# Two mixers and a routed expert layer on one core: attention in pairs of heads, a spread written four tokens at a time, and new places for urgent work in the first stage

## The chip, the core and the metric

One core of one Trainium2 chip runs the whole program. TensorE (PE) multiplies matrices into PSUM, VectorE (DVE) and ScalarE (ACT) work on elements, GpSimd (POOL) gathers rows here, and SyncE (SP) issues most DMAs. Each engine takes its instructions in the order in which they stand in the program. The metric is the time of one execution on the device in microseconds; less is better.

## What is computed

Two blocks over 512 tokens of width 1024, then a last norm in the first block's way of computing:

```python
# first block (rg_lru, peer: helpers)
ada = silu(c) @ w_ada + b_ada                     # sh1, sc1, g1, sh2, sc2, g2
h = rmsnorm(x) * (1 + sc1) + sh1
z = h @ w_in                                      # gate_b, gate_c, xa, xr, gr
y_a = gate_b * causal_dwconv(gate_c * xa)
y_b = rg_lru(causal_dwconv(xr), w_r, w_i, lambda) * gelu(gr)
x = x + g1 * (concat(head_rmsnorm(y_a), head_rmsnorm(y_b)) @ w_out)
x = x + g2 * peer(rmsnorm(x) * (1 + sc2) + sh2)   # 8 heads, the best 16 of 128*128 experts a head
x = rmsnorm(x)
# second block
h = rms_norm(x); proj = h @ w_in
moba = softmax(q k^T / 8 - slope * distance, causal) v * silu(a_z)   # 8 heads of 64
gdn = rms_norm(gated_delta_rule(silu(conv(q, k, v)), g, beta)) * silu(d_z)   # 4 heads of 128
x = x + rms_norm(concat(moba, gdn) @ w_out)
```

With 512 tokens and 3 selectable blocks of 256 keys every past block is selected, so the attention is plain causal attention.

## The kernel before

Large products are made in near fp32: `_split` (L98) copies a tile to fp32r on ACT (wH, hidH, yH, vH, cH) and takes the rest on DVE (wL, hidL, ...), and `_mm3` (L106) makes three matmuls of the parts. `_Weights` (L118) keeps two loaded chunks (wraw) and two split ones ahead. Instructions are put in order by a scheduler when the program is built; `tc.issue_after(x)` makes it keep an instruction behind x.

Stage 1 (`_phase1`, 0 to 217 us) holds x transposed, xT, as 8 chunks of 128 channels x 512 tokens. Squares (L265) are made on ACT and added on DVE (L268), `_token_sums` (ps_ts) sums them over channels on PE, rms and its reciprocal (L163, L164) follow, and four transposes (ps_row) spread it over the partitions. A column of the modulation is one DVE product with accumulation over a 128x1024 tile (wada, L218). xn (L298) is the normed x, hidH and hidL its parts, ps_zp the first product. Then come the convolutions, the gates (tanh, exp, sqrt on ACT, a scan on DVE), the head norms (hnr, rb, ps_row), the product with w_out into four banks at a time, the new xT (L432), and the second norm.

Routing (217 to 365 us) finds the best 16 keys of each head (`_top16` on DVE). Tokens 128 to 511 take the dense way: `spread` (365 to 549 us) makes, from one-hot tiles (ohA, ohB on DVE, L640), a 128x128 table of coefficients for each token on PE (ps_g), ACT copies four tokens at a time into st (L663) and issues a DMA of st to gd in DRAM for every 32 tokens (L665). Beside it PE makes the first 46 of 128 chunks of the experts' inputs (psS, kept in ring). Then 128 steps follow (566 to 1430 us): g4, four chunks of gd for all tokens, is read back (L733), multiplied into ring (L741, DVE), split into cH and cL, and multiplied with the experts' rows (vraw, vH, vL) into pv (L749 to L755). In the first steps the scores of block 0, s, are loaded again (L763) and go through `_top16`.

The second mixer (1430 to 1810 us) weaves two generators of work: A makes the delta rule's inverses (ps_inv, ps_tm, ps_gr, ps_row) and its recurrence (ps_w, vn, ps_s, ps_o), B makes the projections (ps_p; aq, ak, av, az are the attention's), then the attention. PLAN says how many yields of A are woven with how many of B. `attention(j)` works on heads 2j and 2j+1, one after the other: logits ps_l, lg on DVE, exp on ACT, scaling; then for four key blocks transposes (ps_pT), a copy pT and the product ps_ao. G makes the gates of the delta rule and its norm. At the end comes the output projection (ps_m) and the last norm.

Of the kernel before, what the change touches and what calls it, by code (L numbers as in the profile page):

```python
# [20 lines left out]
P = 128  # L21
T = 512
D = 1024
KC = 8
# [6 lines left out]
GN = 4  # L31
LAG = 46
# [81 lines left out]
PLAN = [(18, 8), (18, 60), (12, 24)]  # L114
# [3 lines left out]
class _Weights:  # L118
# [103 lines left out]
def _phase1(k):  # L222

    nc, tc, I = k.nc, k.tc, k.I
    with tc.tile_pool(name="p1", bufs=1, reuse_waits="tile") as p1, \
# [11 lines left out]
        nc.scalar.activation(out=c1, in_=c1, func=AF.Silu)  # L237
        root = p1.tile([P, 1], F32, name="root")
        nc.scalar.activation(out=root, in_=k.eps, func=AF.Sqrt)
# [22 lines left out]
        def add_square(dc):  # L262
# [4 lines left out]
            if dc:  # L267
                nc.vector.tensor_tensor(out=sqs[0], in0=sqs[0], in1=sq, op=OP.add)  # L268

        def rms_row():  # L270

            r = tile_("rms", "rms", 2, (P, 4))
            _rstd(k, r, _token_sums(k, pps, [[sqs[0]]], "np", 2), 1.0 / D)
# [3 lines left out]
        for dc in range(KC):  # L277
            add_square(dc)
# [5 lines left out]
        rps = rms_row()  # L284
# [5 lines left out]
        for dc in range(KC):  # L290
            sc, sh = ada(1, dc), ada(0, dc)
# [5 lines left out]
            with tc.issue_after(mod.ins) if dc else ExitStack():  # L297
                nc.vector.scalar_tensor_tensor(out=t, in0=xT[:, dc, :], scalar=A, in1=row if dc else rps,  # L298
                                               op0=OP.mult, op1=OP.mult)
            with tc.issue_after(k.weights.last.ins) if dc else ExitStack():  # L300
                nc.scalar.activation(out=hH[:, dc, :], in_=t, func=AF.Identity, bias=sh)
# [6 lines left out]
        with tc.issue_after(mod.ins):  # L308
            kc_ = _softplus(k, p1, k.neglam, 4, "lru_k")
# [55 lines left out]
        for j in range(4):  # L365
            nc.scalar.activation(out=tt[j], in_=tt[j], func=AF.Sqrt)
# [13 lines left out]
        def headnorm(ys, gname, m0):  # L380
# [11 lines left out]
            for j, y in enumerate(ys):  # L392
# [4 lines left out]
                nc.vector.scalar_tensor_tensor(out=y, in0=y, scalar=k.col(gname, j, 1), in1=row,  # L397
                                               op0=OP.mult, op1=OP.mult)
# [17 lines left out]
        g1, sh2, sc2 = (ada_group(s, k.conv_end) for s in (2, 3, 4))  # L416
# [3 lines left out]
        for m in range(KC):  # L420
# [14 lines left out]
            add_square(m)  # L435
            xa.append(tile_("xa", ("gate0", "gate1")[m // 4], 4))
            nc.scalar.activation(out=xa[m], in_=xT[:, m, :], func=AF.Copy, scale=A2[:, m:m + 1])
        row = rms_row()
# [92 lines left out]
def _peer(k, psum):  # L531
# [10 lines left out]
    gd = k.dr.tile([NG, P, NK, GT], F32, name="gd")  # L542
# [25 lines left out]
    with ExitStack() as bctx:  # L568
# [63 lines left out]
        def spread(b, iT, gHL):  # L632
# [11 lines left out]
            for gq in range(P // GT):  # L644
                st = po.tile([P, NK, GT], F32, name="st", tag="st", bufs=2)
                for to in range(0, GT, OG):
# [9 lines left out]
                    for j0 in range(0, OG, 4):  # L656
# [73 lines left out]
    for c in range(NK):  # L730
        if c % GN == 0:
            g4 = pc.tile([P, NG, GN, GT], F32, name="g4", tag="g4", bufs=2)
            nc.sync.dma_start(out=g4, in_=gd[:, :, c:c + GN, :].rearrange("g p n t -> p g n t"))  # L733
# [61 lines left out]
def _mixer2(k, psum, pv):  # L795
# [138 lines left out]
    for tb in range(4):  # L934
        for hf in range(2):
# [3 lines left out]
            o = tile_("x3", "lg", 5)  # L939
# [164 lines left out]
    def attention(j):  # L1104
# [13 lines left out]
        nc.scalar.activation(out=az, in_=az, func=AF.Silu)  # L1118
        yield
        po = pps.tile([P, T], F32, name="ps_ao", tag="po", bufs=1)  # L1120
        for hh in range(2):
            h = 2 * j + hh
            off = hh * 64
            rows = slice(off, off + 64)
            slope = 2.0 ** -(h + 1)
            pr = []
            for qb in range(4):
                nk = (qb + 1) * P
# [3 lines left out]
                lg = tile_("lg", "lg", 5)  # L1132
                nc.vector.scalar_tensor_tensor(out=lg[:, 0:nk], in0=C["alibi"][:, 384 - qb * P:512], scalar=slope,
                                               in1=ps[:, 0:nk], op0=OP.mult, op1=OP.add)
                mx = p4.tile([P, 2], F32, name="mx", tag="mx", bufs=6)
                nc.vector.tensor_reduce(out=mx[:, 0:1], in_=lg[:, 0:nk], axis=AX.X, op=OP.max)
                nc.vector.tensor_scalar(out=mx[:, 0:1], in0=mx[:, 0:1], scalar1=-1.0, scalar2=None, op0=OP.mult)
                nc.scalar.activation(out=lg[:, 0:nk], in_=lg[:, 0:nk], func=AF.Exp, bias=mx[:, 0:1],
                                     accum_out=mx[:, 1:2])
                nc.vector.reciprocal(out=mx[:, 1:2], in_=mx[:, 1:2])  # L1140
                nc.vector.tensor_scalar(out=lg[:, 0:nk], in0=lg[:, 0:nk], scalar1=mx[:, 1:2], scalar2=None, op0=OP.mult)
                pr.append(lg)
                yield
            for kb in range(4):
                nq = (4 - kb) * P
                ps = pps.tile([P, T], F32, name="ps_pT", tag="pa", bufs=2)
                for qb in range(kb, 4):
                    nc.tensor.transpose(ps[:, (qb - kb) * P:(qb - kb + 1) * P], pr[qb][:, kb * P:(kb + 1) * P], k.ident)
                pT = tile_("pT", "pT", 3)
                if kb % 2:  # L1150
# [3 lines left out]
                nc.tensor.matmul(out=po[rows, kb * P:T], lhsT=av[:, kb, off:off + 64], rhs=pT[:, 0:nq],  # L1154
                                 start=kb == 0, stop=kb == 3)
                yield
        nc.vector.tensor_tensor(out=az, in0=az, in1=po, op=OP.mult)
        azs.append(az)

    zs = []  # L1160
# [47 lines left out]
    B = chain(delta_inputs(2, ins[1]), delta_inputs(3, ins[1]), *[attention(j) for j in range(4)])  # L1208
    for na, nb in PLAN:
        weave(A, na, B, nb)  # L1210
    for _ in A:
        pass
    G = chain(gates_of_delta(), gated_norm())
    weave(B, 200, G, 10)
# [186 lines left out]
```

## Time and profile before

| | us |
|---|---|
| median of 3 runs | 1864.59 |
| lowest, highest | 1864.06, 1872.85 |
| the profiled execution | 1863.24 |
| its span, first to last instruction | 1861.5 |
| PE busy | 1777.6 (95%) |
| DVE busy | 1480.4 (80%) |
| ACT busy | 831.2 (45%) |

PE is the busiest engine, and its rests are short and of many causes; one of 17.2 us stands out, before the 128 steps. A matmul that streams slowly counts as busy, so the share says nothing of how dense the work is. The clock granted to PE was 0.984 of full speed in the mean.

### The profile page before, as it was taken

How to read it: one execution, taken by the hardware profiler on the slowest of the kernel's cores; microseconds unless marked ns; L12 is line 12 of the kernel's file. 1: busy time of each engine (PE TensorE's matmuls, PEld its weight loads, DVE VectorE, ACT ScalarE, POOL GpSimd, SP SyncE). 2: the span in 40 equal slices, each digit the busy share in tenths (PEclk: the TensorE clock that was granted, in tenths of full speed). 3: DMA queues.
4: the chain of work that ended last, by engine and by line, in shares of the span. 5: the costliest groups of instructions: out<-in, count | busy, mean ns of one | idle time of the engine just before them, and what ended most of it. 6: DMA issues, size and time to landing. Idle time of an engine off the chain costs nothing.

```text
span 1861.5 us, 26283 instructions
## 1 busy us (share of the span) xinstructions
PE 1777.6 (95%) x9613; PEld 1542.2 (83%) x9613; DVE 1480.4 (80%) x3012; ACT 831.2 (45%) x1188; POOL 333.7 (18%) x260
## 2 busy tenths in 40 slices
PE   6999898999968999999999999999999999999988
PEld 5777688999957999999999999988887788767768
DVE  7788699999989978888887888898965774566665
ACT  4464534367863433333333333333335753454452
POOL 0000000000000044544444444455400000000000
PEclk9999999999978999999999999999999999999999
DMA  8355333345669789999999999999962311111022
GB/s 307 124 178 208 121 111 108 122 173 215 259 236 284 235 300 372 356 355 331 346 335 342 334 334 349 336 331 345 352 245 76 112 69 58 57 46 46 12 79 91
DMA packets 153414, 404.53 MB, mean 217 GB/s; under 512 B 12098, under 2 KB 64578, under 8 KB 151748
## 3 DMA queue, kind: packets, MB, share of 16 engines
q1 hardware_dynamic: 114690, 243.45, 38.0%
q0 software_dynamic: 36864, 134.23, 19.8%
q10 hardware_dynamic: 1730, 25.17, 3.5%
q8 instruction: 75, 1.23, 0.3%
q14 instruction: 55, 0.45, 0.1%
HBM read 370.30 MB, written 32.51 MB: 216 GB/s over the span
## 4 chain that ended last, share of the span: by engine, by line
PE 84%; DVE 11%; ACT 3%; issue 1%; DMA 1%; DVEq 0%; ACTq 0%; SPq 0%
PE pv L749 10%; PE pv L752 9%; PE pv L755 9%; PE psS L110 8%; PE psS L109 8%; PE psS L108 8%; PE ps_p L109 3%; PE ps_p L108 3%; PE ps_p L110 3%; PE ps_zp L110 2%; PE ps_zp L109 2%; PE ps_zp L108 2%; PE ps_inv L952 2%; DVE wL L102 2%; PE ps_g L660 2%; DVE ohB L640 1%
## 5 line engine op out<-in xcount | busy, mean ns | idle before, releaser
L101 ACT ACTIVATE wH<-wraw 128x1024 fp32r<-128x1024 f32 x204 | 216.4, 1062 | 417.0 <-PE psS L109 257.8
L108 PE MATMUL psS<-hidH,wH 128*128 128x384 f32 x1024 | 346.9, 339 | 3.5 <-ACT ring L554 3.5
L110 PE MATMUL psS<-hidH,wL 128*128 128x384 f32 x1024 | 346.6, 339 | 3.4 <-DVE wL L102 3.4
L109 PE MATMUL psS<-hidL,wH 128*128 128x384 f32 x1024 | 346.6, 338 | 0.0
L102 DVE TENSOR_TENSOR wL<-wraw,wH 128x1024 fp32r<-128x1024 f32 x204 | 248.9, 1221 | 88.7 <-ACT wH L101 88.3
L707 POOL DMA_INDIRECT row<-uN,uidx x128 | 166.4, 1300 | 831.2 <-DVE cL L102 659.0
L749 PE MATMUL pv<-vH,cH 128*128 128x512 f32 x768 | 223.6, 393 | 17.2 <-ACT vH L101 17.2
L755 PE MATMUL pv<-vH,cL 128*128 128x512 f32 x768 | 237.5, 390 | 0.0
L752 PE MATMUL pv<-vL,cH 128*128 128x512 f32 x768 | 237.4, 390 | 0.0
L101 ACT ACTIVATE cH<-ring 128x384 fp32r<-128x384 f32 x128 | 67.2, 526 | 323.0 <-PE pv L752 301.4
L108 PEld LDWEIGHTS psS<-hidH,wH 128*128 128x128 f32 x1024 | 193.4, 189 | 7.7 <-ACT ring L554 4.5
L716 POOL DMA_INDIRECT row<-vR,vidx x128 | 167.1, 1306 | 172.9 <-DVE acc L722 140.8
L110 PEld LDWEIGHTS psS<-hidH,wL 128*128 128x128 f32 x1024 | 193.3, 189 | 5.2 <-DVE wL L102 4.9
L109 PEld LDWEIGHTS psS<-hidL,wH 128*128 128x128 f32 x1024 | 193.3, 189 | 3.2
L749 PEld LDWEIGHTS pv<-vH,cH 128*128 128x128 f32 x768 | 143.7, 189 | 42.3 <-ACT vH L101 17.4
L709 DVE SCALAR_TENSOR_TENSOR row<-row,h2tok 128x1024 f32<-128x1024 f32 x128 | 154.9, 1220 | 25.5 <-DMA row<-uN,uidx 25.4
L722 DVE SCALAR_TENSOR_TENSOR acc<-row,act,acc 128x1024 f32<-128x1024 f32 x127 | 162.6, 1280 | 11.5 <-DMA row<-vR,vidx 10.7
L102 DVE TENSOR_TENSOR vL<-vraw,vH 128x1024 fp32r<-128x1024 f32 x128 | 156.2, 1221 | 18.5 <-ACT vH L101 18.3
L752 PEld LDWEIGHTS pv<-vL,cH 128*128 128x128 f32 x768 | 144.1, 188 | 31.1
L755 PEld LDWEIGHTS pv<-vH,cL 128*128 128x128 f32 x768 | 144.1, 188 | 31.0
L101 ACT ACTIVATE vH<-vraw 128x1024 fp32r<-128x1024 f32 x128 | 135.8, 1061 | 0.4 <-DMA vraw<-vR 0.2
L663 ACT ACTIVATE st<-ps_g 128x512 f32<-128x512 f32 x96 | 96.2, 1145 | 32.3 <-PE ps_g L660 31.7
(415 smaller groups left out, 2973.0 us busy)
## 6 DMA issues: line engine op xcount, KB each, us to landing
wraw<-uT SPq DMA_DIRECT2D x128, 512.0 KB, 5.9
vraw<-vR SPq DMA_DIRECT2D x128, 512.0 KB, 6.6
wraw<-w_in SPq DMA_DIRECT2D x52, 512.0 KB, 3.5
wada<-wada SPq DMA_DIRECT2D x48, 512.0 KB, 4.9
gd<-st ACTq DMA_DIRECT2D x12, 2048.0 KB, 7.3
g<-gd SPq DMA_DIRECT2D x32, 768.0 KB, 9.2
wraw<-w_out SPq DMA_DIRECT2D x16, 512.0 KB, 3.6
wraw<-w_q SPq DMA_DIRECT2D x8, 512.0 KB, 3.5
```

The source lines that it names most:

```text
L101: copy = nc.scalar.activation(out=H, in_=src, func=AF.Copy)
L102: nc.vector.tensor_tensor(out=L, in0=src, in1=H.bitcast(F32), op=OP.subtract)
L108: nc.tensor.matmul(out=ps, lhsT=lH, rhs=rH, start=start, stop=False)
L109: nc.tensor.matmul(out=ps, lhsT=lH, rhs=rL, start=False, stop=False)
L110: nc.tensor.matmul(out=ps, lhsT=lL, rhs=rH, start=False, stop=stop)
L707: nc.gpsimd.indirect_dma_start(out=row, out_offset=None, in_=I["uN"], in_offset=bass.IndirectOffsetOnAxis(ap=uidx[:, n:n + 1], axis=0))
L709: nc.vector.scalar_tensor_tensor(out=row, in0=row, scalar=1.0, in1=h2tok, op0=OP.mult, op1=OP.mult, accum_out=act0[:, n:n + 1])
L716: nc.gpsimd.indirect_dma_start(out=row, out_offset=None, in_=k.vrows, in_offset=bass.IndirectOffsetOnAxis(ap=vidx[:, n:n + 1], axis=0))
L722: nc.vector.scalar_tensor_tensor(out=k.acc0, in0=row, scalar=act0[:, n:n + 1], in1=k.acc0, op0=OP.mult, op1=OP.add)
L749: nc.tensor.matmul(out=pv[b][h], lhsT=cH[:, bs], rhs=vH[:, h * 512:(h + 1) * 512], start=first, stop=False)
L752: nc.tensor.matmul(out=pv[b][h], lhsT=cH[:, bs], rhs=vL[:, h * 512:(h + 1) * 512], start=False, stop=False)
L755: nc.tensor.matmul(out=pv[b][h], lhsT=cL[:, bs], rhs=vH[:, h * 512:(h + 1) * 512], start=False, stop=last)
```

## The change

In the first stage silu goes ahead of the square root's first use, softplus goes behind the last hidH, the first weights are loaded and split (`first`) before the modulation's first two columns, which wait for the last addition of squares, and each further pair of columns waits for the xn before (`scaled`). At the end of the stage the last square is no longer added on DVE: its sums over channels are made by matmuls of their own and added as 128x4. The gates' r and i use two kinds of banks, gelu waits for the last sqrt and has four buffers, and of the last three groups of modulation columns the third (sh2) waits for the last head norm.

In the spread st is written with four neighbouring tokens in its innermost dimension. gd becomes two tensors, of the first 16 chunks and of the other 112, with a DMA for each. In the second mixer the attention works on both heads of a pair at once, in three generators: the projections, the softmax, and the values, which are woven with the next pair's projections. The last pair's values are woven with the gates. The logits have tiles of their own size.

```diff
-PLAN = [(18, 8), (18, 60), (12, 24)]
+PLAN = [(18, 8), (18, 56), (12, 20)]
...
+    def first(self):
+
+        self.load()
+        self.split()
...
-        def rms_row():
+            if 0 < dc <= last:
+                return nc.vector.tensor_tensor(out=sqs[0], in0=sqs[0], in1=sq, op=OP.add)
+
+        def rms_row(last):
...
+            sums = _token_sums(k, pps, [[q] for q in sqs[0:1] + sqs[last + 1:]], "np", 2)
+            if last < KC - 1:
+                nc.vector.tensor_copy(out=r, in_=sums[:, 4:8])
+                nc.vector.tensor_tensor(out=r, in0=r, in1=sums[:, 0:4], op=OP.add)
+                sums = r
+            _rstd(k, r, sums, 1.0 / D)
...
-        rps = rms_row()
+        k.weights.first()
+        with tc.issue_after(added.ins):
+            for s in (1, 0):
+                ada(s, 0)
+        rps = rms_row(KC - 1)
...
+            if dc < KC - 1:
+                with tc.issue_after(scaled.ins):
+                    for s in (1, 0):
+                        ada(s, dc + 1)
...
-            H, L = k.weights.get()
+            with tc.issue_after(scaled.ins):
+                H, L = k.weights.get()
...
-        with tc.issue_after(mod.ins):
+        with tc.issue_after(mod.ins), tc.issue_after(high.ins):
             kc_ = _softplus(k, p1, k.neglam, 4, "lru_k")
...
-                ps = bank("gp", 2)
+                ps = bank(("gp", "np")[g], 2)
...
-                g = tile_("gg", "gg", 2)
-                nc.scalar.activation(out=g, in_=ps, func=AF.Gelu_apprx_tanh)
+                g = tile_("gg", "gg", 4)
+                with tc.issue_after(gate.ins):
+                    nc.scalar.activation(out=g, in_=ps, func=AF.Gelu_apprx_tanh)
...
-        g1, sh2, sc2 = (ada_group(s, k.conv_end) for s in (2, 3, 4))
+        g1, sc2, sh2 = (ada_group(s, after) for s, after in ((2, k.conv_end), (4, k.conv_end), (3, k.normed)))
...
-    gd = k.dr.tile([NG, P, NK, GT], F32, name="gd")
+
+    gd = [k.dr.tile([NG, P, n, GT], F32, name="gd%d" % n) for n in (NF, NK - NF)]
...
-                        nc.scalar.activation(out=st[:, :, o:o + 4].rearrange("p n t -> p t n"), in_=ps,
+                        nc.scalar.activation(out=st[:, :, o:o + 4], in_=ps.rearrange("p t n -> p n t"),
                                              func=AF.Copy, scale=1.0 / GSCALE)
-                nc.scalar.dma_start(out=gd[(b - 1) * (P // GT) + gq], in_=st)
+                for part, cs in zip(gd, (slice(0, NF), slice(NF, NK))):
+                    nc.scalar.dma_start(out=part[(b - 1) * (P // GT) + gq], in_=st[:, cs, :])
...
+            src, c0 = (gd[0], c) if c < NF else (gd[1], c - NF)
+            nc.sync.dma_start(out=g4, in_=src[:, :, c0:c0 + GN, :].rearrange("g p n t -> p g n t"))
...
+    def values(j, st):
+        aq, ak, av, az, pr = st[j]
+        po = pps.tile([P, T], F32, name="ps_ao", tag="po", bufs=1)
+        for kb in range(4):
+            nq = (4 - kb) * P
+            pts = []
+            for hh in range(2):
...
+                pts.append(pT)
+            yield
+            for rows, pT in zip(halves, pts):
+                nc.tensor.matmul(out=po[rows, kb * P:T], lhsT=av[:, kb, rows], rhs=pT[:, 0:nq],
                                  start=kb == 0, stop=kb == 3)
...
+    def attention():
+
+        st = {}
+        yield from projections(0, st)
+        for j in range(4):
+            yield from softmax(j, st)
+            if j < 3:
+                a, b = values(j, st), projections(j + 1, st)
+                for n in range(5):
+                    next(a)
+                    yield
+                    next(b)
+                    yield
...
-    weave(B, 200, G, 10)
+    weave(last[0], 9, G, 9)
```

How the instructions move is shown at three places. The first is DVE at the start of stage 1, from the fifth addition of squares on; sq_100 is the sum, A a column of the scale. Before:

```order
L268 TENSOR_TENSOR sq_100<-sq_100,sq_117 128x512
L218 SCALAR_TENSOR_TENSOR wada,ada<-wada,cb 128x1024
L268 TENSOR_TENSOR sq_100<-sq_100,sq_120 128x512
L218 SCALAR_TENSOR_TENSOR wada,ada<-wada,cb 128x1024
L294 SCALAR_TENSOR_TENSOR A_142<-ada,cols,G_123 128x1
L292 TENSOR_TENSOR ada<-ada,cols 128x1
L102 TENSOR_TENSOR wL<-wraw,wH 128x1024
L164 RECIPROCAL rms<-rms 128x4
L102 TENSOR_TENSOR wL<-wraw,wH 128x1024
L218 SCALAR_TENSOR_TENSOR wada,ada<-wada,cb 128x1024
L298 SCALAR_TENSOR_TENSOR xn<-xT,A_142,ps_row 128x512
```

And now:

```order
L275 TENSOR_TENSOR sq_100<-sq_100,sq_117 128x512
L275 TENSOR_TENSOR sq_100<-sq_100,sq_120 128x512
L103 TENSOR_TENSOR wL<-wraw,wH 128x1024
L224 SCALAR_TENSOR_TENSOR wada,ada<-wada,cb 128x1024
L170 RECIPROCAL rms<-rms 128x4
L310 SCALAR_TENSOR_TENSOR A_156<-ada,cols,G_123 128x1
L224 SCALAR_TENSOR_TENSOR wada,ada<-wada,cb 128x1024
L308 TENSOR_TENSOR ada<-ada,cols 128x1
L314 SCALAR_TENSOR_TENSOR xn<-xT,A_156,ps_row 128x512
```

The additions are no longer parted by a wada product, the reciprocal of rms comes behind one wL and one wada, and one wada product stands between it and xn.

The second is PE in the mixer, at the stretch from 1665 us on in the trace before, where the second head's products of one pair (ps_ao), the next logits (ps_l) and the inputs of a new group of inverses (ps_row, ps_gr) meet. Before:

```order
L182 MATMUL ps_row<-ca,gcum 128x128 x4
L182 MATMUL ps_row<-ca,ksc 128x128 x4
L1154 MATMUL ps_ao<-pT,av 64x256
L1130 MATMUL ps_l<-ak,aq 128x128
L966 MATMUL ps_gr<-kT 128x128 x4
L1154 MATMUL ps_ao<-pT,av 64x128
L1130 MATMUL ps_l<-ak,aq 128x256
L1130 MATMUL ps_l<-ak,aq 128x384
L182 MATMUL ps_row<-ca,ksc 128x128 x4
L966 MATMUL ps_gr<-kT 128x128 x4
L1130 MATMUL ps_l<-ak,aq 128x512
L108 MATMUL ps_p<-hidH,wH 128x512
```

And now, at the same group of inverses:

```order
L188 MATMUL ps_row<-ca,ksc 128x128 x4
L1194 MATMUL ps_ao<-pT,av 64x512 x2
L1184 MATMUL ps_pT<-ca,lg 128x128
L991 MATMUL ps_gr<-kT 128x128 x4
L1184 MATMUL ps_pT<-ca,lg 128x128 x5
L110 MATMUL ps_p<-hidL,wH 128x512
L111 MATMUL ps_p<-hidH,wL 128x512
L109 MATMUL ps_p<-hidH,wH 128x512
L110 MATMUL ps_p<-hidL,wH 128x512
L111 MATMUL ps_p<-hidH,wL 128x512
```

Projections (ps_p) now stand between the products of the attention, and the two ps_ao of a pair stand next to each other.

The third is PE at the first step of the delta rule's recurrence, near 1780 us in the trace before. Before:

```order
L952 MATMUL ps_inv<-kv,XT 128x128 x4
L952 MATMUL ps_inv<-XT,kv 128x128 x4
L1075 MATMUL ps_w<-S,nwT 128x128 x3
L1148 MATMUL ps_pT<-ca,lg 128x128 x2
L1075 MATMUL ps_w<-S,nwT 128x128
L1148 MATMUL ps_pT<-ca,lg 128x128 x2
L1083 MATMUL ps_s<-vn,ik 128x128 x4
```

And now:

```order
L984 MATMUL ps_tm<-ca,vT 128x128 x4
L1194 MATMUL ps_ao<-pT,av 64x128 x2
L977 MATMUL ps_inv<-kv,XT 128x128 x4
L977 MATMUL ps_inv<-XT,kv 128x128 x4
L1100 MATMUL ps_w<-S,nwT 128x128 x4
L1108 MATMUL ps_s<-vn,ik 128x128 x4
L1115 MATMUL ps_o<-S,qT 128x128
```

The transposes of the last softmax no longer stand between the steps of the recurrence; they are woven with the gates ahead of it.

## Rows read from the trace of the kernel before

**Rows 1.** Table of stretches: PE, weight loads, DVE, ACT, POOL busy us; clock; DMA.
```profile
365.00:530.00 165.00, 165.00 (x1367) 156.10 (x1366) 156.72 (x313) 122.52 (x143) 0.00 (x0) 1.00 0.57 210
530.00:550.00 20.00, 12.25 (x116) 9.73 (x114) 19.25 (x47) 15.32 (x17) 0.00 (x0) 0.68 0.61 245
550.00:566.00 16.00, 0.26 (x1) 0.26 (x2) 10.31 (x60) 2.21 (x4) 0.00 (x0) 0.50 0.83 296
...
1663.00:1720.00 57.00, 52.05 (x276) 38.32 (x277) 36.25 (x86) 24.18 (x44) 0.00 (x0) 1.00 0.14 47
1720.00:1810.00 90.00, 81.95 (x514) 61.59 (x513) 58.96 (x138) 45.44 (x83) 0.00 (x0) 1.00 0.13 42
```

**Rows 2.** Who waited for whom, PE: us in total, times, longest.
```profile
PE pv L749 <- ACT vH L101: 17.2, 1, 17.2
PE ps_ts L156 <- DVE sq L268: 8.3, 2, 5.4
...
PE ps_zp L108 <- ACT hidH L301: 3.3, 1, 3.3
...
PE ps_p L108 <- DVE aq L1106: 2.5, 1, 2.5
PE ps_pT L1148 <- DVE lg L1141: 2.2, 2, 1.8
...
PE ps_row L182 <- ACT rb L394: 1.6, 1, 1.6
```

**Rows 3.** Timeline of PE, start: start, us, what, in brackets idle before.
```profile
22.54 2.07 PE L108 MATMUL ps_zp<-hidH,wH 128*128 128x512 f32 x4 [3.30 <-ACT hidH L301]
```

**Rows 4.** Timeline of DVE, start.
```profile
14.81 0.68 DVE L268 TENSOR_TENSOR sq<-sq,sq 128x512 f32<-128x512 f32 x1
...
17.90 0.17 DVE L164 RECIPROCAL rms<-rms 128x4 f32<-128x4 f32 x1
```

**Rows 5.** Timeline of ACT, start.
```profile
6.30 1.28 ACT L209 ACT_TABLE_LOAD   x1
```

**Rows 6.** Timeline of PE near 115 us.
```profile
115.40 0.50 PE L108 MATMUL ps_zp<-hidH,wH 128*128 128x512 f32 x1 [1.53 <-ACT wH L101]
...
117.03 0.58 PE L110 MATMUL ps_zp<-hidH,wL 128*128 128x512 f32 x1 [0.90 <-DVE wL L102]
```

**Rows 7.** Timeline of DVE near 112 us, the first of three products.
```profile
112.32 1.21 DVE L218 SCALAR_TENSOR_TENSOR wada<-wada,cb 128x1024 f32<-128x1024 f32 x1
```

**Rows 8.** Who waited for whom, DVE, from 365 to 550 us.
```profile
DVE wL L102 <- ACT wH L101: 6.5, 7, 1.9
```

**Rows 9.** Costliest groups of the page: busy us, mean ns of one, idle before.
```profile
L663 ACT ACTIVATE st<-ps_g 128x512 f32<-128x512 f32 x96 | 96.2, 1145 | 32.3 <-PE ps_g L660 31.7
```

**Rows 10.** Timeline of ACT in the mixer, a plain copy.
```profile
1785.41 0.58 ACT L1153 ACTIVATE pT<-ps_pT 128x512 f32<-128x512 f32 x1
```

**Rows 11.** DMA queues from 550.5 to 555.6 us: packets, MB, share of 16 engines.
```profile
q10 hardware_dynamic: 128, 2.10, 108.8%
q1 hardware_dynamic: 15, 0.02, 0.8%
```

**Rows 12.** Timeline of DVE in the gap before the 128 steps.
```profile
558.17 0.49 DVE L455 MAX8 ts<-s 128x8 f32<-128x128 f32 x2 [4.29 <-DMA s<-sc]
...
563.16 1.50 DVE L741 TENSOR_TENSOR ring<-ring,g 128x384 f32<-128x384 f32 x3 [1.40 <-DMA g<-gd]
```

**Rows 13.** Timeline of DVE in the mixer, logits just ahead of aq.
```profile
1674.32 0.67 DVE L1133 SCALAR_TENSOR_TENSOR lg<-cb,ps_l 128x512 f32<-128x512 f32 x1
```

**Rows 14.** Timeline of PE in the recurrence, a step without other work.
```profile
1796.24 1.16 PE L1083 MATMUL ps_s<-vn,ik 128*128 128x128 f32 x8 [0.78 <-DVE vn L1078]
```

**Rows 15.** Groups of PE by line, 1430 to 1810 us.
```profile
L1130 PE MATMUL ps_l<-ak,aq 64*128 64x128 f32 (+3 forms) x64 | 23.6, 468 | 0.0
L1154 PE MATMUL ps_ao<-pT,av 128*64 128x512 f32 (+3 forms) x64 | 22.2, 451 | 1.6 <-ACT pT L1153 1.6
```

More of the change, by code (lines that the diff above doesn't have):

```diff
@@ L31 @@
 GN = 4
+NF = 16
 LAG = 46
@@ L236, in _phase1 @@
             nc.sync.dma_start(out=xT[:, 2 * q:2 * q + 2, :], in_=I["xT"][:, 2 * q:2 * q + 2, :])
-        nc.scalar.activation(out=c1, in_=c1, func=AF.Silu)
+        silu = nc.scalar.activation(out=c1, in_=c1, func=AF.Silu)
         root = p1.tile([P, 1], F32, name="root")
-        nc.scalar.activation(out=root, in_=k.eps, func=AF.Sqrt)
+        with tc.issue_after(silu.ins):
+            nc.scalar.activation(out=root, in_=k.eps, func=AF.Sqrt)
         nc.scalar.dma_start(out=k.cd, in_=c1)
@@ L260, in _phase1, with add_square @@
         sqs = []
-        def add_square(dc):
+        def add_square(dc, last):
             sq = tile_("sq8", ("th", "gc")[dc // 4], 4)
@@ L277, in _phase1 @@
         for dc in range(KC):
[L278 removed]
+            added = add_square(dc, KC - 1)
         G1 = p1.tile([P, 8], F32, name="G1")
@@ L1102, in recurrence, with projections @@
             yield
-    def attention(j):
+    def projections(j, st):
         aq, ak = tile_("aq", "aq", 2), tile_("ak", "ak", 2)
@@ L1118, in attention, with softmax @@
         nc.scalar.activation(out=az, in_=az, func=AF.Silu)
+        st[j] = aq, ak, av, az, [[], []]
         yield
[L1120 to L1128, printed above, removed]
+    halves = [slice(0, 64), slice(64, 128)]
+    def softmax(j, st):
+        aq, ak, av, az, pr = st[j]
+        for qb in range(4):
+            nk = (qb + 1) * P
+            pss = []
+            for rows in halves:
                 ps = pps.tile([P, T], F32, name="ps_l", tag="pa", bufs=2)
@@ L1131, in attention @@
                                  start=True, stop=True)
[L1132 to L1136, printed above, removed]
+                pss.append(ps)
@@ new lines, in softmax @@
+            for hh, ps in enumerate(pss):
+                lg = tile_("lg", "lg%d" % qb, 2, (P, nk))
+                nc.vector.scalar_tensor_tensor(out=lg, in0=C["alibi"][:, 384 - qb * P:512],
+                                               scalar=2.0 ** -(2 * j + hh + 1), in1=ps[:, 0:nk],
+                                               op0=OP.mult, op1=OP.add)
+                mx = p4.tile([P, 2], F32, name="mx", tag="mx", bufs=10)
+                nc.vector.tensor_reduce(out=mx[:, 0:1], in_=lg, axis=AX.X, op=OP.max)
@@ L1142, in attention @@
-                pr.append(lg)
+                nc.vector.tensor_scalar(out=lg, in0=lg, scalar1=mx[:, 1:2], scalar2=None, op0=OP.mult)
+                pr[hh].append(lg)
                 yield
-            for kb in range(4):
-                nq = (4 - kb) * P
+    def values(j, st):
+        aq, ak, av, az, pr = st[j]
+        po = pps.tile([P, T], F32, name="ps_ao", tag="po", bufs=1)
[3 more added lines that the diff above has]
+            for hh in range(2):
@@ L1153, in attention @@
                     nc.scalar.activation(out=pT[:, 0:nq], in_=ps[:, 0:nq], func=AF.Copy)
-                nc.tensor.matmul(out=po[rows, kb * P:T], lhsT=av[:, kb, off:off + 64], rhs=pT[:, 0:nq],
+                pts.append(pT)
+            yield
+            for rows, pT in zip(halves, pts):
+                nc.tensor.matmul(out=po[rows, kb * P:T], lhsT=av[:, kb, rows], rhs=pT[:, 0:nq],
                                  start=kb == 0, stop=kb == 3)
-                yield
+            yield
         nc.vector.tensor_tensor(out=az, in0=az, in1=po, op=OP.mult)
         azs.append(az)
+    def attention():
[9 more added lines that the diff above has]
+                    next(b)
+                    yield
+                for _ in a:
+                    yield
+                assert next(b, None) is None
+        st["last"] = values(3, st)
+        last.append(st["last"])
+    last = []
     zs = []
@@ L1207, in _mixer2 @@
     A = chain(heads(ins[0]), heads(ins[1]), recurrence())
-    B = chain(delta_inputs(2, ins[1]), delta_inputs(3, ins[1]), *[attention(j) for j in range(4)])
+    B = chain(delta_inputs(2, ins[1]), delta_inputs(3, ins[1]), attention())
     for na, nb in PLAN:
@@ L1212, in _mixer2 @@
         pass
+    for _ in B:
+        pass
     G = chain(gates_of_delta(), gated_norm())
-    weave(B, 200, G, 10)
+    weave(last[0], 9, G, 9)
     for _ in G:
```

31 lines of the change are left out of this document (13 added, 18 removed).

## The prediction

> **What bounds the kernel now.** I read the table of stretches first, to see where TensorE (PE) rests. From 365 to 530 us it is busy all the time; from 530 to 566 us it works 12.5 of 36 us, and the 16 us before 566 stand almost still; in the last part of the second mixer it rests 4.95 us (1663 to 1720) and 8.05 us (1720 to 1810) [rows 1]. PE has no fewer matmuls after the change, so what there is to win are these rests and those of the first stage. The list of PE's waits names them: 17.2 us once for vH before the first pv, 8.3 us in two waits for the sum of squares, 3.3 us for the first hidH, 1.6 us for rb, 2.5 us for aq, 2.2 us for lg [rows 2]. Then I went to each place with the timeline, and last to the DMA queues of the gap. The sums are made against the profiled execution, 1863.24 us (span 1861.5 and 1.7 around it), 1.35 us under the median of 1864.59.
>
> **Stage 1, the start.** PE has its first real matmul at 22.54, after a rest of 3.30 us for hidH [rows 3]. On VectorE (DVE) a wada product, 1.22 us, stands ahead of the last square's addition, which therefore starts at 14.81; the reciprocal of rms runs at 17.90 [rows 4]. Now the additions stand in one piece: one step of 1.14 us less. On ScalarE (ACT) one table load of 1.28 us [rows 5] less stands ahead of the squares, and none ahead of rms: 1.2 less. Between the last addition and xn DVE had four large instructions (wada, wL, wL, wada) and has three (wL, wada, wada); half of a step counts, 0.6, since wL also waits for a load. Together -3.0 us. It is nothing where the first weights arrive late, and with the whole step -3.6: 0 to -3.6.
>
> **Stage 1, the rest.** At 115 us PE waits 1.53 us for wH and 0.90 us for wL [rows 6], behind three wada products from 112.32 on [rows 7] and tables that ACT changes between sqrt and gelu. Both go to later places, where the weights are two chunks ahead: -2.0 (0 to -2.4). The head norm's reciprocal no longer stands behind three wada products, and the wait for rb is 1.6 [rows 2]: -1.5 (0 to -1.6). At the end of the stage PE waits 2.9 of the 8.3 us for the last addition [rows 2], which stands behind a wL; it is replaced by four more small matmuls, a copy and an add of 128x4: -1.0. Against it stand five wada products, near 6 us, right ahead of the first xT. Those xT are due only when the first half's four banks are wanted again, a good 5 us later by PE's order, so I take nothing; uncovered it is up to 3 us: +2.0 to -1.3. Sum of the stage: -7.5.
>
> **The spread, 365 to 549 us.** DVE is the bound there, and rests 6.5 us for wH [rows 8], which stands on ACT behind st copies of 1145 ns, 96 of them [rows 9]. A plain 128x512 copy out of PSUM takes 0.58 us on ACT [rows 10]. The new st writes four neighbours and reads PSUM in strides of 512 bytes; no row shows that form. Bounds: 0.58 us, or the same and more (rival C). I take about 0.65, nearer to the plain copy, since the scattered write was what set st apart from it: wH then comes sooner, and I give 2.5 of the 6.5 us (0 to -4.5). The Trainium skill (SBUF — State Buffer, Door 1) says that SBUF gives full speed to accesses that stay in one line of 16 bytes, which four fp32 fill; by it the write is cheap and the term stands. [...]
>
> **The gap to the first pv, 549 to 566 us.** gd's 2 MB write holds the first g4, which lands at 563.16 [rows 12]. With the first 256 KB as a tensor of their own, g4 may be issued some 5 us sooner. But the other 1.75 MB run right behind them. While gd was written (550.5 to 555.6), ACT's queue q10 moved 2.10 MB and SP's q1 0.02 MB, although two s loads of 128 KB had been issued on q1 [rows 11]. One of these kept DVE idle 4.29 us, until 558.17; DVE's top-16 work on it ended at 561.76, and only the last 1.40 us before the ring product were g4's own [rows 12]. DVE's order is unchanged there: s, top-16, ring. So g4's 5 us shrink to 1.4 while the s loads come no sooner; that and two quicker st at the end (0.5) give about -2.0 (-1.0 to -5.0). The Trainium skill (DMA: Bandwidth & Descriptors, Queues, rings and completion order) says that a DMA engine changes between queues after every packet. By it s and g4 would share with the write and the term would be -4; the rows disagree, 0.02 MB against 2.10.
>
> **The second mixer.** Before, each head does softmax, then transposes, copies and ao, and near 1663 to 1676 us these stand with ps_row and ps_gr and no projections between them. The next ps_p waits 2.5 us for a bank that DVE frees with aq [rows 2], behind logits of 0.67 us each and decay work [rows 13]. In the new order projections of the next pair stand between: -2.5, and -1.0 for short waits on pT. The last pair's softmax moves in front of the gates' projections, so that PE's wait for lg, 2.2 [rows 2], loses its place, with some 0.8 of the same kind beside it: -3.0. The recurrence loses what filled its steps (pT and ao between ps_w and ps_s), and a bare step waits 0.78 [rows 14]: +1.0. Of the other 7 us of rest in these two stretches I take a fifth: -1.5. Sum -7.0. Bounds: all 13.0 us of rest won [rows 1], or new stalls of 4: -13 to +4. The long product loop between and the output projection are not touched.
>
> **Sum.** -7.5 - 2.5 - 2.0 - 7.0 = -19.0, so 1863.2 - 19.0 = 1844.2, and 1845.5 against the median. I say 1845.
>
> **Rivals.**
> A. Pairs overlap in the array. The two ps_l of a pair use the upper and the lower 64 rows of PE's inputs, the two ps_ao 64 columns each, and now often stand next to each other (14 neighbours among 32 ps_l, 6 among 32 ps_ao). Their matmuls take 23.6 and 22.2 us [rows 15]. If neighbours ran at once, half of 23.6 x 28/32 and of 22.2 x 12/32 would go: 14.5 us; since each fp32 matmul shows as two passes in sequence, a quarter is likelier, 7. Before has no such neighbours to show it. Time 1838, at best 1831. The Trainium skill (TensorEngine Tiling (Array Packing), Key Properties) has it that different tiles execute in parallel.
> B. The mixer wins little. Both halves' logits, maxima and scalings now come to DVE together, at 0.67 us an instruction for 512 columns [rows 13], and PE waits for lg and for banks as before. For it: DVE works strictly in order. Against it: the projections between. With nothing won there -12, 1852; with 1 to 3 us of new stalls 1854.
> C. Slower: the strided read makes st slower. ACT is busy 122.5 of 165 and 15.3 of 20 us [rows 1]; the 47 us left are 0.49 us for each of 96 copies, so at 1.63 us ACT is full. Each further 0.1 us costs 9.6 us. Without the spread's gain, the other 16.5 us are used up at 1.80 us, and at 2.0 us the time is 1882. Against it: the writes of st get shorter in any case.
> D. The change doesn't do what it says: the start stays bound by loads, five wada delay xT, the rest of gd holds g4 and s, and the mixer's rests only shift. Stage 1 gives -2, the gap -1, the others nothing: 1860.
>
> **Numbers.** Chances: forecast 0.54 (own range 1837 to 1853), A 0.16, B 0.14, C 0.08, D 0.08. A difference under 0.5%, 9.3 us, can't be told from none. Faster than that: nearly all of the forecast, A, and over a third of B: 0.75. Within: the rest of B and of the forecast, and most of D: 0.16. Slower: C and a little of D: 0.09. The range 1830 to 1860 leaves out C and the tails of A and D.
>
> **What would show it.** First ps_zp at 19 to 20 us; no wait over 1 us near 115; st at 0.6 to 0.7 us; q1 nearly idle while the rest of gd is written, and DVE's wait for s before the ring product still there; no ps_p wait of 2.5 us in the mixer; ps_l and ps_ao as costly as now. Wrong if st takes over 1.2 us, if PE's rests from 1663 to 1810 are as long as now, or if ps_l falls by a quarter (A).

## The result, and the profile after

The changed kernel takes 1841.85 us (median of 4 runs, 1841.42 to 1845.08) against 1867.34 us for the kernel before in the same comparison (4 runs, 1864.06 to 1872.85): 0.9864 times the time, 95% interval 0.9834 to 0.9894, so faster by 25.5 us in the medians. The two profiled executions differ by less: spans of 1861.5 and 1840.5 us, 21.0 us, and against this the steps are held. (The traced execution of before is one of its quicker ones, as the clocks among the experiments show.) The forecast was 1845. The number came out near; the sum behind it did not come out as it was made.

Where the 21.0 us came from is read off by the start of the same piece of work in both timelines:

| Start of (of a last one: end) | before, us | after, us | won so far |
|---|---|---|---|
| first ps_zp (stage 1) | 22.54 | 19.10 | 3.4 |
| first ps_q (end of stage 1) | 215.66 | 213.01 | 2.7 |
| first ps_g (spread) | 377.85 | 377.83 | 0.0 |
| last ps_g | 548.57 | 547.58 | 1.0 |
| first pv (end of the gap) | 565.74 | 563.60 | 2.1 |
| last pv (mixer begins) | 1430.0 | 1426.85 | 3.2 |
| end | 1861.48 | 1840.49 | 21.0 |

Stage 1, spread and gap together hold 2.1 us when the product loop begins. From the last pv to the end it is 431.48 us before and 413.64 after, 17.8 us less: in this pair of profiles nearly all was won in the second mixer.

The table of stretches of after (columns as in [rows 1], whose stretches these are):

```profile
365.00:530.00 165.00, 165.00 (x1369) 156.03 (x1368) 158.08 (x313) 88.87 (x144) 0.00 (x0) 1.00 0.57 211
530.00:550.00 20.00, 11.53 (x116) 9.43 (x114) 19.79 (x54) 8.87 (x15) 0.00 (x0) 0.74 0.65 256
550.00:566.00 16.00, 2.40 (x6) 1.92 (x7) 11.41 (x60) 3.64 (x6) 0.00 (x0) 0.50 1.07 341
...
1663.00:1720.00 57.00, 55.43 (x333) 42.47 (x331) 40.29 (x88) 24.25 (x47) 0.00 (x0) 1.00 0.14 47
1720.00:1810.00 90.00, 84.30 (x599) 71.65 (x599) 60.57 (x127) 42.64 (x83) 0.00 (x0) 1.00 0.19 65
```

ACT's work in the spread fell from 122.5 to 88.9 us, and DVE, as full as before, still sets its pace. PE's rests from 1663 to 1810 us are 1.57 and 5.70 us, 7.3 where there were 13.0; the stretches don't hold quite the same work in both kernels, since after is further on.

PE's waits of after, all those over 2 us that the argument is about (us in total, times, longest; [rows 2] is the same view of before):

```profile
PE pv L774 <- ACT vH L102: 16.0, 1, 16.0
...
PE ps_ts L162 <- DVE sq L275: 5.1, 1, 5.1
...
PE ps_zp L111 <- DVE wL L103: 3.9, 2, 3.2
...
PE ps_gp L369 <- ACT wH L102: 2.5, 1, 2.5
PE ps_s L1108 <- DVE vn L1103: 2.3, 3, 0.8
```

The waits of ps_p for aq and of ps_pT for lg are gone. One wait is new, 3.2 us of ps_zp for a wL. And this is the group of ps_l and ps_ao (PE by line, 1430 to 1810 us, as [rows 15]; busy us, mean ns of one, idle before):

```profile
L1194 PE MATMUL ps_ao<-pT,av 128*64 128x512 f32 (+3 forms) x64 | 20.4, 458 | 0.3 <-ACT pT L1190 0.3
L1158 PE MATMUL ps_l<-ak,aq 64*128 64x128 f32 (+3 forms) x64 | 14.8, 482 | 0.0
```

The same 64 ps_l, none of them quicker (482 ns against 468), keep PE busy for 14.8 instead of 23.6 us. So they ran beside each other, which an experiment tests below.

### The profile page after: what moved, and what is told of

Read it like the earlier page. It is cut to its first block, busy times and chain, and to the rows that moved or that the text cites. A ratio compares the mean times of both kernels' runs of the same rounds, so it can differ in the third digit from the quotient of the medians.

```text
span 1840.5 us, 26310 instructions
## 1 busy us (share of the span) xinstructions
PE 1766.4 (96%) x9621; PEld 1537.4 (84%) x9621; DVE 1481.3 (80%) x3013; ACT 781.4 (42%) x1182; POOL 334.5 (18%) x260
## 4 chain that ended last, share of the span: by engine, by line
PE 83%; DVE 11%; ACT 3%; DMA 1%; issue 1%; SPq 0%; DVEq 0%; ACTq 0%
PE pv L774 10%; PE pv L777 10%; PE pv L780 10%; PE psS L111 9%; PE psS L109 9%; PE psS L110 9%; PE ps_p L109 3%; PE ps_p L110 3%; PE ps_p L111 3%; PE ps_inv L977 2%; PE ps_g L683 2%; PE ps_zp L109 2%; PE ps_zp L111 2%; PE ps_zp L110 2%; DVE wL L103 2%; PE ps_ao L1194 1%
## 5 line engine op out<-in xcount | busy, mean ns | idle before, releaser
L103 DVE TENSOR_TENSOR cL<-ring,cH 128x384 fp32r<-128x384 f32 x128 | 71.0, 555 | 54.9 <-ACT cH L102 54.6
```

The lines of the kernel that those rows point to most:

```text
L103: nc.vector.tensor_tensor(out=L, in0=src, in1=H.bitcast(F32), op=OP.subtract)
```

## The experiments

Each kernel was measured beside the kernel before on the same chip, in groups of up to four. A ratio is the time over that of before. The median of before itself moved from 1867 to 1873 us between groups, so kernels of different groups are compared by their ratios. The first question was which of the three parts of the change won.

**The attention part alone** (before, with the new attention and PLAN; nothing of stage 1 and the spread):

```diff
-PLAN = [(18, 8), (18, 60), (12, 24)]
+PLAN = [(18, 8), (18, 56), (12, 20)]
...
-    def attention(j):
+    def projections(j, st):
```

> The kernel before with the attention's part alone (pairs of heads, values woven with projections, the new PLAN). After stands 18.1 us ahead of before between the first pv's end and the end of the program (3.15 at the last pv, 21.0 at the end). Theory: this part alone gives 17 to 18.5 us, about 1845 against a profiled 1863, of which 8.8 + 1.8 us are ps_l and ps_ao running two at a time (ps_l group 14.8 us busy instead of 23.6) and the rest fewer waits. Rival (the prediction's sum): it gives 7 us, and the rest came from elsewhere.

1848.41 us, ratio 0.9898 (0.9861 to 0.9934); span 1843.5, 18.0 under that of before. From the last pv to the end it takes 413.7 us, what the whole change takes (413.6). So the attention is most of the gain, and in these profiles nearly all of it.

**Stage 1 alone, and the spread with both gd tensors alone:**

```diff
+        k.weights.first()
+        with tc.issue_after(added.ins):
```

> The kernel before with the first stage's part alone. In the changed kernel the first ps_q stands 2.65 us earlier, the first psS 1.56 us, the first ps_g 0.0 us. Theory: what the stage wins is lost again before the spread begins at 378 us (half-clock stretches and the bound DVE), so 0 to 2 us in all, 1862 to 1864 profiled. Rival (the prediction's sum): 7.5 us, 1856.

```diff
-                        nc.scalar.activation(out=st[:, :, o:o + 4].rearrange("p n t -> p t n"), in_=ps,
+                        nc.scalar.activation(out=st[:, :, o:o + 4], in_=ps.rearrange("p t n -> p n t"),
```

> The kernel before with st in runs of four and the two gd tensors alone. Theory: st takes 0.60 us, the last ps_g comes 1 us earlier, the first pv 2 to 2.5 us earlier, the last pv about 3 us earlier because the half-clock stretch after the gap is shorter: 1860 to 1861 profiled. Rival (the prediction's sum): 4.5 us, 1859. Second rival: nothing in the spread, 1.4 from the gap.

1867.52 us, ratio 0.9994 (0.9974 to 1.0014), and 1866.34 us, 0.9985 (0.9964 to 1.0007). Neither can be told from before. In the profiled executions they begin the mixer 5.4 and 5.1 us sooner than before and end it 5.6 and 6.7 us later. Their mixer is the old one, yet takes 442.5 and 443.2 us where before's takes 431.5. The table of stretches of the spread kernel shows what differs, the granted clock (third number from the end):

```profile
1430.00:1500.00 70.00, 68.27 (x342) 54.33 (x341) 51.13 (x117) 52.44 (x77) 0.00 (x0) 0.93 0.24 79
1500.00:1600.00 100.00, 99.69 (x547) 83.00 (x546) 57.48 (x93) 39.01 (x57) 0.00 (x0) 1.00 0.21 67
1600.00:1700.00 100.00, 96.40 (x483) 74.08 (x482) 61.38 (x142) 45.41 (x73) 0.00 (x0) 0.93 0.15 48
1700.00:1810.00 110.00, 102.11 (x616) 76.80 (x615) 68.41 (x161) 54.10 (x99) 0.00 (x0) 0.98 0.13 44
```

In before the same four stretches had 0.98, 1.00, 0.98 and 1.00. Stretches at the half clock (1.2 GHz) make 34.1 us of this mixer and 6.8 of before's, leaving out the last one, at the end of the program. At half clock half of a stretch is lost at most: (34.1 - 6.8) / 2 = 13.7 us bounds the effect, and the 11.8 us lie within it. That the clock made the difference is read from one profile each, not tested.

The clocks of whole executions point the same way. Beside these kernels before ran 19 times, and its spans go from 1859.3 us at a granted clock of 0.985 to 1873.9 at 0.975. The traces of the two parts, at 0.979 and 0.978, are set here against one of before at 0.984. A straight line through the 47 spans and clocks of this group, with one slope for all kernels (1.3 us for each 0.001 of the clock), gives an estimate at equal clock: against before, attention -17.8 us, stage 1 -3.1, spread -1.7, each to about 1.5 us, together -22.6. The 30 executions of the group in which after was timed again put the whole change at -22.8. So the two parts do seem to give something; that they leave the clock itself as it is, is assumed.

**Do the pairs overlap?** After, with the second head's logits made from the first head's rows (its own logits are left out), so that both ps_l of a pair use the same rows of the array:

```diff
-            for rows in halves:
+            for rows in (halves[0], halves[0]):
```

> The changed kernel, but the second head of each pair computes its logits from the first head's rows 0 to 63 of aq and ak (the second head's own logits are left out); order and sizes of all instructions are the same. Both ps_l of a pair then use the same 64 rows of PE. Theory: neighbours run at once only because they use different rows, so ps_l goes back from 14.8 to 23.6 us busy and the kernel takes 7 to 9 us more than the changed one, about 1850. Rival: the ps_l got cheaper by their place in the order, and nothing changes, 1842.

1847.40 us, ratio 0.9891 (0.9854 to 0.9927). The timeline of PE has neighbouring ps_l as one row (start, length, number). Of after:

```profile
1577.28 0.70 PE L1158 MATMUL ps_l<-ak,aq 64*128 64x128 f32 x4
1581.29 0.92 PE L1158 MATMUL ps_l<-ak,aq 64*128 64x256 f32 x4
1587.09 1.13 PE L1158 MATMUL ps_l<-ak,aq 64*128 64x384 f32 x4
```

and of the kernel with the same rows:

```profile
1574.31 0.92 PE L1158 MATMUL ps_l<-ak,aq 64*128 64x128 f32 x4
1578.53 1.34 PE L1158 MATMUL ps_l<-ak,aq 64*128 64x256 f32 x4
1584.77 1.77 PE L1158 MATMUL ps_l<-ak,aq 64*128 64x384 f32 x4
```

Four instructions (two products in two passes each) take 1.13 us in different rows and 1.77 in the same. Over all of them:

```profile
L1158 PE MATMUL ps_l<-ak,aq 64*128 64x128 f32 (+3 forms) x64 | 22.0, 459 | 0.0
```

22.0 against 14.8 us is 7.2 more, and the mixer takes 420.2 instead of 413.6, 6.6 more. Nothing else was changed, but this trace has one more stretch of 3.4 us at half clock in its mixer, at most 1.7 us of loss. That leaves at least 4.9 of the 6.6 us for the overlap: it is there, and it stands on the path to the end. The Trainium skill (TensorEngine Tiling (Array Packing), Key Properties) has it that different tiles execute in parallel; the rows agree.

**What the weave is worth.** After, with a pair's values finished before the next pair's projections begin:

```diff
                 a, b = values(j, st), projections(j + 1, st)
-                for n in range(5):
-                    next(a)
-                    yield
-                    next(b)
-                    yield
...
                 for _ in a:
                     yield
-                assert next(b, None) is None
+                for _ in b:
+                    yield
```

> The changed kernel with the values of a pair and the projections of the next pair one after the other instead of woven. The two heads of a pair still stand side by side, so neighbours still run at once. The prediction gave the weaving 3.5 us (waits for aq's bank and for pT). Theory: it is worth 3 to 6 us, since PE's rests without it are also followed by stretches at half clock. Rival: the pairs alone make the gain, 0 to 1 us.

1856.77 us, ratio 0.9949 (0.9928 to 0.9971). Its mixer takes 427.1 us, 13.5 more than after's: over twice the 3 to 6 us that I had expected, and nearly four times the 3.5 of the prediction. The stretches 1663 to 1720, 1720 to 1755, 1755 to 1775, 1775 to 1790 and 1790 to 1810 us of it:

```profile
1663.00:1720.00 57.00, 53.96 (x327) 39.16 (x325) 38.29 (x84) 24.22 (x47) 0.00 (x0) 1.00 0.08 29
1720.00:1755.00 35.00, 31.29 (x198) 27.48 (x199) 14.67 (x22) 9.97 (x14) 0.00 (x0) 1.00 0.09 31
1755.00:1775.00 20.00, 17.61 (x126) 14.01 (x124) 16.54 (x50) 14.93 (x26) 0.00 (x0) 1.00 0.28 106
1775.00:1790.00 15.00, 9.71 (x42) 5.24 (x40) 11.32 (x29) 10.47 (x20) 0.00 (x0) 0.77 0.19 70
1790.00:1810.00 20.00, 19.20 (x139) 16.06 (x138) 10.80 (x18) 6.77 (x16) 0.00 (x0) 1.00 0.15 54
```

PE rests 15.2 us there, 8.0 more than in after. The last logits now come behind the projections (the last ends at 1774.77, the last ps_p at 1755.39; in after the last logits start at 1730.8), where nothing is left to fill the softmax. ps_ao takes 23.6 us and ps_l 16.4, 3.2 and 1.6 more than in after. These three add up to 12.8 of the 13.5 us. How far the 0.77 of the clock has a share was not separated.

**Stage 1 mended.** The same kernel as after was timed again beside three variants (the first text is its expectation), one of which holds the last of the three groups of modulation columns until four new xT are made:

```diff
-        g1, sc2, sh2 = (ada_group(s, after) for s, after in ((2, k.conv_end), (4, k.conv_end), (3, k.normed)))
+        g1, sc2 = (ada_group(s, k.conv_end) for s in (2, 4))
...
+            if m == 3:
+                sh2 = ada_group(3, added)
```

> The changed kernel once more, to see how far its executions differ and to compare the next three with. Theory: the rests of PE decide by small shifts whether a stretch at half clock follows, so single executions differ by a few us; median 1841 to 1845. Rival: it repeats within 0.5 us.

> The changed kernel with the sh2 columns (eight wada products) held behind the fourth new xT instead of behind the last head norm. In the changed kernel three of them stand ahead of a wL at 169.7 us, for which PE waits 3.23 us, and five ahead of the first xT, for which it waits 1.16 and then 0.83 us more. Theory: these 5.2 us of rests go, the first ps_q comes 4 to 5 us earlier, and about 3 us of it reach the end: 1839. Rival: DVE is the bound in the routing, and the gain is lost there, 1842.

After again: 1839.19 us, ratio 0.9843 (0.9827 to 0.9859), just clear of the 0.9898 (0.9861 to 0.9934) of the attention alone; the first timing, 0.9864 (0.9834 to 0.9894), is not. In its second profile after has the first ps_g at 373.68, the first pv at 560.01 and the last at 1423.24 us, 6.5 us sooner than with the attention alone. Both then take 413.7 us to the end, so here the gain of the other parts arrives whole: spans of 1837.0 and 1843.5. Mended: 1838.39, 0.9823 (0.9801 to 0.9845). PE's waits of the mended kernel between 160 and 215 us:

```profile
PE ps_q L109 <- ACT hidH L470: 1.5, 1, 1.5
PE ps_row L188 <- DVE rms L170: 1.0, 1, 1.0
PE ps_zp L111 <- DVE wL L103: 0.5, 1, 0.5
```

The wait for wL fell from 3.2 to 0.5 us and that for xT (1.2) is gone, ps_q begins 6.2 us sooner than in after's second profile and the mixer 3.9 us sooner. Of that the spans keep 0.3 us: the mixer took 417.3 us instead of 413.7, with 13.7 us at half clock instead of 3.4. The intervals overlap, so this is no proven better version. Its clocks were lower, though, 0.982 and 0.983 against 0.984 and 0.985; its one execution at 0.988 spans 1827.9 us, and all five of after 1837.0 or more.

**The gap.** Three ideas to win the time between spread and loop: let the first gd tensor land before the other 1.75 MB are written (eight idle ACT copies between them), the same with the mended stage 1, and hold the top-16 work of heads 2 to 7 behind the first ring product.

```diff
+                    for n in range(8):
+                        with tc.issue_after(kept.ins):
+                            kept = nc.scalar.activation(out=idle, in_=st[:, 0:NF, :].rearrange("p n t -> p (n t)"), func=AF.Copy)
+                with tc.issue_after(kept.ins):
+                    nc.scalar.dma_start(out=gd[1][row], in_=st[:, NF:, :])
```

> The changed kernel with eight plain copies of 128x512 into an unused tile on ACT (about 4.8 us) between the last gd DMA of 256 KB and the last one of 1.75 MB. Theory: the loads of s and g4 wait for the big write, so with the write later s no longer keeps DVE idle for 4.59 us, g4 lands near 555, the ring product comes near 556.5 instead of 561.0 and the end 4 to 5 us earlier: 1837 to 1838. Rival (queues change after every packet, so s and g4 were not held by the write): the ring product stays at 561 and nothing changes, 1842.

> Both edits of the two runs before, on the changed kernel. Theory: the gains add up, 7 to 8 us, 1834 to 1835. Rival: only the gap's gain is seen, since the routing takes the first stage's, 1838.

```diff
-            with tc.issue_after(k.after_spread.ins):
+            with tc.issue_after((k.first_ring if c else k.after_spread).ins):
```

> The changed kernel with the top-16 work of block 0's heads 2 to 7 held behind the first ring product; two s loads of 128 KB still stand ahead of g4 on SP's queue, but DVE no longer needs them before the ring product. Theory (the write holds every load behind it): the ring product then starts when g4 lands, and g4's data move only after the 1.75 MB are written, so it lands near 560 to 561 and little is won, 0 to 1 us. Rival (s was what held the ring product): it starts at 557, 4 us earlier.

The delay: 1852.02 us, 0.9907 (0.9889 to 0.9924), and with the mend 1844.69, 0.9861 (0.984 to 0.9883): slower than after by 0.6% (the first). It doesn't answer the question as put, because the scheduler moved six s loads and their top-16 ahead of the ring product; pv then waited 22.8 us. The hold: 1842.37 us, 0.9871 (0.9847 to 0.9895). Its ring product starts 11.9 us after the last ps_g instead of 13.4 and waits for g alone (timeline of DVE):

```profile
556.21 1.03 DVE L766 TENSOR_TENSOR ring<-ring,g 128x384 f32<-128x384 f32 x2 [8.91 <-DMA g<-gd]
```

So s was the last of two that waited behind the write, as forecast; with s out of the way it is g4. The time, as expected, isn't better for it. Both together, and both with the mend and thirteen copies:

> As e_hold, and with the eight plain copies on ACT (5.3 us) between the last 256 KB and the last 1.75 MB. In the run before with these copies the scheduler had put six s loads and their top-16 work ahead of the ring product, so that it told nothing. Theory: nothing is written while g4 is read, it is issued near 548.5 (some 4.5 us after the last ps_g) and lands 4 to 6 us later; the first pv comes 10 to 12 us after the last ps_g instead of 16.0, and the time is 4 to 6 us less than that of the changed kernel. Rival: g4's own 512-byte pieces are slow, and it lands no sooner: 0 to 1 us.

> The changed kernel with the sh2 columns behind the fourth new xT, the top-16 work of heads 2 to 7 behind the first ring product, and thirteen plain copies on ACT (8.5 us) instead of eight before the last 1.75 MB. With eight copies the ring product came 7.8 us after the last ps_g instead of 13.4, but the write then held the rows of experts (vraw), and the first pv came 15.6 us after it. Theory: the write holds whatever is loaded behind it; begun 3 us later, it lets g4 and the first vraw through, and the first pv comes 11 to 12 us after the last ps_g; 4 us less than with the sh2 edit alone, 1834 to 1835. Rival: the loop's first steps pay it back, as they did for the top-16 work held back alone (its pv came 1.5 us earlier and the last pv did not): 1838 to 1840.

1846.37 us, 0.9887 (0.9862 to 0.9912), and 1840.76, 0.9837 (0.9816 to 0.9858). With hold and delay the ring product starts 7.8 us after the last ps_g, but pv waits on. Timeline of ACT in that kernel, then SP's wait for the write, and the issues of the first vraw (at 547.37) and of the write (at 549.61) with their times to landing:

```profile
558.39 1.06 ACT L102 ACTIVATE vH<-vraw 128x1024 fp32r<-128x1024 f32 x1 [5.03 <-DMA gd<-st]
...
562.50 1.06 ACT L102 ACTIVATE vH<-vraw 128x1024 fp32r<-128x1024 f32 x1 [3.06 <-DMA vraw<-vR]
```

```profile
SPq L767 <- DMA gd<-st: 10.1, 1, 10.1
...
vraw<-vR SPq DMA_DIRECT2D x1, 512.0 KB, 6.4
...
gd<-st ACTq DMA_DIRECT2D x1, 1792.0 KB, 8.6
```

The first vH waits 5.03 us for the write itself, not for its data: the first vraw lands near 553.8, the write near 558.2. The second vraw is issued only then (558.29; L767 is its line). As I read the program, tiles of the loop lie where st lay and can't be written before the write has read it; in after, too, the second vraw is issued at 557.28, just behind the write's landing near 557.2. So what I expected of thirteen copies, that the write held vraw's data, was a misreading: a later write makes the first vH later. pv starts 15.6 us after the last ps_g (after: 16.0), and with thirteen copies 16.6. The delay frees s and g4 and pays with the tiles that wait for the write to end. No version beats after beyond its interval.

## Why the prediction was right, and which steps failed

**Start, -3.0:** -3.4, right. The first ps_zp is at 19.10, its wait for hidH 2.22 instead of 3.30 us.

**115 us, -2.0:** right; no wait over 1 us is left there (0.72 at 105 us is the nearest). The wait for rb is gone, as said, and in place of the last addition (2.8 us) PE waits 0.5 for a square.

**End of the stage, "so I take nothing":** failed. I took five wada products for covered by PE's order, and did not see the three that come before them. Timeline of DVE in after:

```profile
168.55 1.22 DVE L224 SCALAR_TENSOR_TENSOR wada<-wada,cb 128x1024 f32<-128x1024 f32 x1
...
169.69 1.22 DVE L103 TENSOR_TENSOR wL<-wraw,wH 128x1024 fp32r<-128x1024 f32 x1
...
180.18 1.22 DVE L224 SCALAR_TENSOR_TENSOR wada<-wada,cb 128x1024 f32<-128x1024 f32 x1 [0.51 <-DMA wada<-wada]
...
181.33 1.40 DVE L454 SCALAR_TENSOR_TENSOR xT<-ps_zp,ada,xT 128x512 f32<-128x512 f32 x2
```

and of PE, the two that waited for these:

```profile
170.97 0.80 PE L111 MATMUL ps_zp<-yH,wL 128*128 128x512 f32 x1 [3.23 <-DVE wL L103]
...
182.22 0.47 PE L109 MATMUL ps_zp<-yH,wH 128*128 128x512 f32 x1 [1.16 <-DVE xT L454]
```

The wL stands behind three wada (from 166.26) and starves PE for 3.23 us; the xT are late by 1.16, inside the bound of 3 that I had set. PE's waits listed from 160 us to the first ps_q sum to 8.2 us, against 7.2 before. The stage gave 2.7 us of its 7.5 at ps_q, and by the first ps_g nothing is left in this pair of profiles. Until there after has 23.9 us at half clock (among them 3.4 us each from 171.0, 184.6 and 324.6, the first two behind these waits) and before 17.1, which can cost 3.4. The second profile of after, with 17.1 us as before, has its first ps_g at 373.68, 4.2 us sooner than before. So the loss on the way to ps_g belongs to this one execution; that the clock is its cause is not tested.

**Spread, -2.5:** st takes 597 ns, near the plain copy [rows 10]; rival C is out:

```profile
L686 ACT ACTIVATE st<-ps_g x96: 579/597/617, 378.5 to 547.6; 128x512 f32<-128x512 f32 x96
```

(start of the group's row: shortest, median, longest ns, and first and last start.) But the step from it to 2.5 us was too generous. DVE's waits from 378 to 550 us:

```profile
DVE ohA L663 <- PE ps_g L683: 3.7, 9, 0.9
DVE wL L103 <- ACT wH L102: 1.4, 3, 0.7
```

In the same stretch of before it waits 5.5 us for wH (6.5 from 365 us on, [rows 8], which is 2.3 in after). That is 4.1 less, but its waits for ps_g are 3.7, 1.9 more than before. From the first to the last ps_g the spread takes 169.75 us instead of 170.72: -1.0 (170.38 in after's second profile).

**Gap, -2.0:** -1.15, with its mechanism as described. The DMA queues from 550.5 to 555.6 us (as [rows 11]) and DVE's timeline:

```profile
q10 hardware_dynamic: 116, 1.59, 96.4%
q1 hardware_dynamic: 39, 0.04, 2.2%
```

```profile
557.51 0.49 DVE L477 MAX8 ts<-s 128x8 f32<-128x128 f32 x2 [4.59 <-DMA s<-sc]
...
561.02 1.48 DVE L766 TENSOR_TENSOR ring<-ring,g 128x384 f32<-128x384 f32 x3
```

The ring product no longer waits for g (1.40 before, [rows 12]) and stands 2.1 us sooner, 1.0 of it from the spread; s is still held. By the Trainium skill (DMA: Bandwidth & Descriptors, Queues, rings and completion order) an engine changes queues after each packet, and a packet holds some 9 to 17 descriptors. I had taken each of the profile's 128 pieces of the write for such a packet, and 0.04 MB against 1.59 for a disagreement. But 128 pieces on 16 engines are 8 for each (an estimate), which may well be one packet; then page and trace agree. No run here shows where a packet ends.

**Mixer, -7.0:** -17.8, the term that was mis-sized, by 10.8 us. What I counted, PE's rests, I had nearly right: 13.0 became 7.3 us in the two stretches, -5.7; over the whole mixer, where the same work is compared, 24.2 became 19.6, -4.6. What I had put into rival A came on top of it: ps_l -8.8 and ps_ao -1.8 us busy. ps_p is 2.9 less too (196.2 and 193.2 us), for a reason that no run shows. These three make 13.5 us; PE's busy time fell by 13.3 in all, which with the 4.6 is the whole term. By the sign that I had set (ps_l down by a quarter), the forecast's mechanism was wrong here and A's right. The failed step is A's "a quarter is likelier": I let two passes of an fp32 product speak against overlap, and the pairs in different rows overlap wholly enough to save 37% of the group. So A was no rival at all: it excludes nothing of the forecast, and belonged in the sum with a size between 0 and 14.5. Not all of the 8.8 is overlap: with the same rows ps_l takes 22.0 us, 1.6 less than before. That ps_ao's 1.8 is overlap was not tested by itself.

**Why the number still held:** stage, spread and gap gave 2.1 us of 12.0, the loop between gave 1.0 that I had not counted, and the mixer 10.8 more than forecast. 2.14 + 1.01 + 17.84 = 21.0, against 19.0. Two errors of opposite sign cancelled, which was luck. Rivals B and D are out for the mixer; on the first stage D's -2 was nearer than my -7.5 (2.7 at ps_q, 3.1 by the estimate at equal clock).

## What to carry to other kernels

Where a change puts two matmuls next to each other that use different rows of the array, count their overlap in the sum, and compare a group's busy time before and after. (Its count times its mean is more than its busy time even without such pairs: 30.0 against 23.6 us for the ps_l of before.) A gain made early in a long kernel can be covered by the granted clock of one execution: look at the start of the same work at five or six places, and compare executions of equal clock. And before splitting a write to set a load free, list all that waits for the rest of it: the loads behind it and the tiles that come free only when it has ended.

## What was not expected of the hardware

- Two ps_l of different row halves start 7 ns apart (1577.279 and 1577.286 us) and the group of 64 shrinks from 23.6 to 14.8 us, though each is an fp32 product of two passes.
- An ACT copy that reads PSUM in strides of 512 bytes and writes runs of four fp32 takes 597 ns, against 580 for the plain copy [rows 10] and 1145 for the one that wrote single ones [rows 9]: the write was the cost, not the read.
- The same mixer code had 6.8 us at half clock in before and 34.1 in the spread kernel, and took 11.8 us longer; 19 executions of before span 1859.3 us at a clock of 0.985 to 1873.9 at 0.975. Gains of 4 to 6 us at the mixer's begin were gone at the end of such profiles, and arrived whole where the clock was equal.
- Loads of 128 KB (s) that were issued before the large write of the kernel with the delay took 2.0 to 2.2 us to land, and 5.9 and 7.8 behind the 1.75 MB of after.
